# A table load, two chunks on single banks and an order of four products in a two-layer encoder

## The chip, the cores and the metric

The kernel runs on one core of a Trainium2 chip. TensorE (PE in the profile) multiplies, VectorE (DVE) and ScalarE (ACT) prepare operands and take results out of PSUM, GpSimd (POOL) does small things, SyncE (SP) issues nearly all transfers. The metric is device time in microseconds. The kernel before took 2409.35 us, the median of 3 runs (2408.86 to 2410.06).

## The reference

Two layers over 256 tokens of width 2048, in float32. Each layer is a token mixer and a gated MLP, both behind an RMSNorm and added to the residual; a last RMSNorm follows.

```
for layer in range(2):
    hn = rmsnorm(h, norm_mix_g[layer])
    mix = mlstm_mixer(hn, ...) if layer == 0 else hgrn_mixer(hn, ...)
    h = h + mix
    h = h + conv_glu(rmsnorm(h, norm_ffn_g[layer]), ...)
return rmsnorm(h, final_g)
```

The mLSTM mixer projects to q, k, v, an output gate and 32 input and forget gates, runs a matrix memory in both directions for 8 heads, and projects back. The HGRN mixer projects to q, v, an output gate and two forget gates, runs a gated linear recurrence in both directions for 16 heads, and projects back. conv_glu is `(gelu(conv3(u_a)) * u_v) @ w_down` with 5504 inner columns.

## The kernel before

**Products in two parts.** Every big product is made from float32 operands that are split into a rounded high part and the rest: `x = xh + xl`, `w = wh + wl`, and `xh wh + xh wl + xl wh` is accumulated. ACT casts wh from the raw weights (L161, L190 in the first chunk), DVE subtracts to get wl (L162, L191). A piece is 1024 columns of wh and wl; four pieces can be live. SP brings the raw weights, two pieces to a transfer.

**Chunks and pairs.** `stream` walks a list of chunks. A token chunk ("tm", L366 to L368) makes 512 output columns for both halves of the tokens, three products of 512 columns for each half and slice of 128 inputs. A feature chunk ("fm", L382 and L385) makes 256 output features f = 0, 1 for all tokens: for each slice k of 16 and each f a high product (wh against xh and xl side by side, 512 columns) and a low one (wl against xh, 256 columns). These two are called a pair of products below; a slice is two of them. With `turns=1`, which the mLSTM query chunks have, slice 1 is sent high, high, low, low instead (L374, L376): a turn. A `Pair` chunk (`stream_pair`, L253) makes the MLP's projections by Strassen's scheme with the sums c11 to c22 and m1, m6, m7.

**PSUM.** Eight banks: two double banks (`double`, for chunks and the rows of a pair) and four single ones (`aux`, for m1, m6, m7, transposes pz, small sums pr, and the heads' products pa, pd, py). A tile is handed out again when its readers are done. A pair takes both double banks; at its end DVE adds them into hx (L1154), 1024 columns at a time.

**Side work.** `side` holds generators for the heads, the norms and the gates; `tick` lets them issue instructions between products. `tc` then orders each engine's instructions by a simulated timeline, so a changed dependency changes orders, too; instructions on one engine run in that order.

**The start.** ACT issues the transfer of the first slice of x (hx, 128 KB) and the first 16 columns of the small parameters (pp, 8 KB). ACT's first activation needs its function table, whose load stands ahead of it. SP issues the first chunk's weights and the rest of x in groups of 1, 2, 4, 4 and 4 slices (`FIRST`). `prepare(k)` splits slice k of x (L390 on ACT, L391 on DVE) and of the weights. TensorE fills the time with `IDLE` products of ones (L1183), each of which the trace shows as two records.

**HGRN heads.** A head gathers q and k for seven levels (DVE), then sends small products: pa (64 rows) and pd (32 rows, L914), and later py (L962). They stand in TensorE's queue between the projections' products.

**The end.** The down projection of the last 11 slices of the MLP makes output columns 0 to 1023 as a pair, 1024 to 1535 as a token chunk, and 1536 to 2047 as the last chunk. The last chunk does its last seven slices for the first half of the tokens, then for the second, 21 products each (L353 to L355), and `half` (L563 to L576) scales and writes out each half.

Of the kernel before, what the change touches and what calls it, by code (L numbers as in the profile page):

```python
# [15 lines left out]
P = 128  # L16
# [35 lines left out]
AHEAD = 3  # L52
SQUARES = (10, 12, 14, 15)
FIRST = (0, 1, 2, 4, 8, 12, 16)
IDLE = 11

QUAD = 32
LEVELS = (1, 2, 4, 8, 16, 32, 64)
# [5 lines left out]
def trunk_kernel(ctx, tc, xT, x_d, fg_d, pp_d, cst_d, sel_d, w_gate, w_first, w_aq, w_ak, w_av, w_ao, w_aout,  # L64
# [30 lines left out]

    class Side:
        def __init__(self):
            self.now, self.jobs = 0.0, []

        def push(self, gen, stay=False):  # L100
            self.jobs.append([gen, self.now, stay])
# [24 lines left out]

    class Chunk:
        def __init__(self, kind, src, nk, x, done, before=None, last=False, turns=0):
            self.last, self.turns = last, turns
            self.kind, self.src, self.nk, self.x, self.done, self.before = kind, src, nk, x, done, before  # L130
            self.width = {"fm": 256, "tm": 512, "first": 512}[kind]

# [32 lines left out]
    def first_chunk(ch, norm, fetch):  # L165

        raws = [slot(k, "first").bitcast(F32) for k in range(KT)]
        nc.scalar.dma_start(hx[:, 0:1], xT[:, 0:1])
        nc.scalar.dma_start(pp[:, 0:KT], pp_d[:, 0:KT])
        for k0, k1 in zip(FIRST, FIRST[1:]):  # L170
            for k in range(k0, k1):
                nc.sync.dma_start(raws[k], ch.src[:, k * 512:(k + 1) * 512])
            if k0:
                nc.sync.dma_start(hx[:, k0:k1], xT[:, k0:k1])
        rg = wpool.tile([P, 2048], F32, tag="raw", bufs=RAW, name="raw")
        nc.sync.dma_start(rg[:, :512], w_gate)
        late(cst[:, 0:C_LV], cst_d[:, 0:C_LV])
        late(cst[:, C_LV:C_LV + P], sel_d)
        late(pp[:, KT:], pp_d[:, KT:])
        pin = tc.keep_in_program_order  # L180
        d = double("mm")
        ps = [d[:, 0:512], d[:, 512:1024]]
        ws = {}

        def prepare(k):
            norm.take(k, hT[k], pin)
            if k % 2 == 0:
                ws[k] = [wpool.tile([P, 1024], F32R, tag=n, bufs=WB, name=n) for n in ("wh", "wl")]
            wh, wl = [w[:, k % 2 * 512:k % 2 * 512 + 512] for w in ws[k - k % 2]]
            pin(act.copy(wh, raws[k]))  # L190
            pin(dve.tensor_tensor(wl, raws[k], wh.bitcast(F32), ALU.subtract))  # L191
        for k in range(AHEAD):
            prepare(k)
        for k in range(KT):
            if k + AHEAD < KT:
                prepare(k + AHEAD)
            if k in SQUARES:
                for i, q in enumerate(SQUARES):
                    if q == k:
                        ch.squares(i)  # L200
            if k >= KT - LOOK:
                fetch()
            x, (wh, wl) = norm.xs[k], [w[:, k % 2 * 512:k % 2 * 512 + 512] for w in ws[k - k % 2]]
            for t in range(2):
                xh, xl = x[:, t * P:(t + 1) * P], x[:, T + t * P:T + (t + 1) * P]
                pe.matmul(ps[t], xh, wh, start=k == 0, stop=False)
                pe.matmul(ps[t], xh, wl, start=False, stop=False)
# [12 lines left out]
        ch.done(ps + [pg])  # L220
# [98 lines left out]
    def stream(chunks):  # L319
# [10 lines left out]
        for ch in chunks[1:]:  # L330
            if ch.before:
                ch.before()
            if ch.kind == "pair":
# [2 lines left out]
                    return ready.pop(0)  # L336
                stream_pair(ch, take)
                continue
            d = double("mm")
            ps = [d[:, 0:512], d[:, 512:1024]]  # L340
            k = 0
            while k < ch.nk:
                fetch()
# [15 lines left out]
                for kk in range(n):  # L359
                    x = ch.x(k)  # L360
                    st, sp = k == 0, k == ch.nk - 1
                    if ch.kind != "fm":
                        c = slice(kk * 512, (kk + 1) * 512)
                        for t in range(2):
                            xh, xl = x[:, t * P:(t + 1) * P], x[:, T + t * P:T + (t + 1) * P]
                            pe.matmul(ps[t], xh, wh[:, c], start=st, stop=False)  # L366
                            pe.matmul(ps[t], xh, wl[:, c], start=False, stop=False)  # L367
                            pe.matmul(ps[t], xl, wh[:, c], start=False, stop=sp)  # L368
                        side.tick(1.3)
                    else:  # L370
                        if k == 1 and ch.turns:
                            cs = [slice(kk * ch.width + f * P, kk * ch.width + (f + 1) * P) for f in range(2)]
                            for f in range(2):
                                pe.matmul(ps[f], wh[:, cs[f]], x, start=False, stop=False)  # L374
                            for f in range(2):
                                pe.matmul(ps[f][:, 0:T], wl[:, cs[f]], x[:, 0:T], start=False, stop=False)  # L376
                            side.tick(0.65)
                            k += 1
                            continue
                        for f in range(len(ps)):  # L380
                            c = kk * ch.width + f * P
                            pe.matmul(ps[f], wh[:, c:c + P], x, start=st, stop=False)  # L382
                            if f:
                                side.tick(0.325 * len(ps))
                            pe.matmul(ps[f][:, 0:T], wl[:, c:c + P], x[:, 0:T], start=False, stop=sp)  # L385
                    k += 1
# [439 lines left out]
    def hgrn(norm, nxt, after):  # L826
# [60 lines left out]
        def head(hd):  # L887
# [54 lines left out]
            for i in reversed(range(FINE)):  # L942
                product(pd[:, (i + 1) * 64:(i + 2) * 64], *ms[i], QUAD)
            product(pd[:, 0:64], ks, q, QUAD)
            act.copy(AD, both(pd[:, 0:64]))
            for i in range(FINE):
                dve.copy_predicated(AD, mask[i], both(pd[:, (i + 1) * 64:(i + 2) * 64]))
# [41 lines left out]
        for qd in range(BH // 4):  # L989
# [14 lines left out]
            for i in range(6):  # L1004
                if i == 3:
                    chunks.append(Chunk("tm", w_bv[qd], KT, norm.x, done_v))
                def done_i(ps, i=i, qd=qd):
                    for f in range(2):
                        r = 2 * i + f
                        take(4 * qd + r // 3, r % 3, ps[f])  # L1010
                chunks.append(Chunk("fm", w_bq[6 * qd + i], KT, norm.x, done_i, begin if not chunks else None))
            for j in range(4):
                heads[4 * qd + j]["qd"] = four
            chunks.append(Chunk("tm", w_bg[qd], KT, norm.x, done_g))
# [15 lines left out]
    def ffn(layer, norm, nxt):  # L1030
# [78 lines left out]
        for part, (f0, nf) in enumerate(PARTS):  # L1109
# [55 lines left out]
            if final:  # L1165
# [5 lines left out]
                for c in (2, 3):  # L1171
                    chunks.append(Chunk("tm", w_last[c - 2], nf, GT.get, done))
                chunks[-1].last, chunks[-1].half = True, nxt.half
        return chunks, begin, stack.close


# [16 lines left out]
    def swap():  # L1193
        close0()
        b()
    c[0].before = swap
    chunks += c
    chunks += f1
    stream(chunks)
# [97 lines left out]
```

## Time and profile before

| | |
|---|---|
| median of 3 runs | 2409.35 us |
| profiled execution, its own time | 2410.66 us |
| its span | 2408.9 us |
| mean granted TensorE clock | 0.999 |

The span reaches from the first to the last instruction of the profile, the time holds what lies around it as well: 1.76 us here. In the timeline's rows stand the start in us, the duration, the engine, the line of the kernel, the operation and its tiles, and in brackets how long the engine had been idle and what ended that. Matmuls are pipelined: the distance from one start to the next is the pace, and the durations, whose ends are modelled, are longer than it. PEld is TensorE's weight load.

By the timeline the first chunk ends near 34 us, HGRN's projections begin at 1102.53 us, and the last chunk's second half begins at 2395.42 us.

### The profile page before, as it was taken

The numbers are of one execution on the slowest core, as the hardware profiler recorded it, in microseconds if no ns is written. First come the engines' busy times: TensorE is split into PE (matmuls) and PEld (weight loads), VectorE is DVE, ScalarE is ACT, GpSimd is POOL, SyncE is SP. The second block draws the span as 40 slices with busy tenths as digits, with TensorE's granted clock in tenths as the row PEclk, the third lists the DMA queues.
The fourth block names the chain that finished last, engine by engine and source line by source line (L and its number), as shares of the span: only waits on it lengthen the run. The fifth ranks groups of instructions, "written<-read, shape, count | busy, mean of one in ns | idle before, by whom it ended". The sixth has DMA issues, their size and how long they took to land.

```text
span 2408.9 us, 34452 instructions
## 1 busy us (share of the span) xinstructions
PE 2391.3 (99%) x13163; PEld 1998.5 (83%) x13163; DVE 2017.9 (84%) x3009; ACT 1396.1 (58%) x2062; POOL 162.9 (7%) x223
## 2 busy tenths in 40 slices
PE   9999999999999999999999999999999999999998
PEld 7888888788887888888888888888878888888896
DVE  7766667998889887997888888886898889988886
ACT  6655455666456555665555555556566556654664
POOL 0100000000000000001222222220000000000000
PEclk9999999999999999999999999999999999999999
DMA  7655554555555555565555455455555555555564
GB/s 294 200 173 173 190 175 175 194 182 201 192 192 192 192 194 208 165 204 178 173 171 167 171 176 171 162 175 177 190 177 208 181 205 191 193 191 192 192 210 140
DMA packets 67061, 451.01 MB, mean 187 GB/s; under 512 B 7744, under 2 KB 8384, under 8 KB 15440
## 3 DMA queue, kind: packets, MB, share of 16 engines
q1 hardware_dynamic: 64800, 442.32, 52.9%
q0 software_dynamic: 1232, 5.31, 1.0%
q8 instruction: 103, 1.69, 0.3%
q10 hardware_dynamic: 864, 1.19, 0.2%
q14 instruction: 62, 0.51, 0.1%
HBM read 446.62 MB, written 2.16 MB: 186 GB/s over the span
## 4 chain that ended last, share of the span: by engine, by line
PE 92%; DVE 6%; issue 1%; ACT 1%; DMA 0%; POOLq 0%; ACTq 0%; POOL 0%; DVEq 0%
PE c L253 44%; PE mm L382 10%; PE mm L366 7%; PE mm L367 7%; PE mm L368 7%; PE m L253 5%; PE mm L385 5%; DVE wl L162 3%; PE pt L1062 1%; PE pn L731 1%; PE pd L914 1%; PE py L962 1%; DVE T L235 1%; PE pz L476 0%; PE pa L914 0%
## 5 line engine op out<-in xcount | busy, mean ns | idle before, releaser
L162 DVE TENSOR_TENSOR wl<-raw,wh 128x1024 fp32r<-128x1024 f32 (+1 forms) x837 | 967.5, 1167 | 227.5 <-ACT wh L161 226.7
L161 ACT CAST wh<-raw 128x1024 fp32r<-128x1024 f32 (+1 forms) x837 | 829.0, 1001 | 567.7 <-PE c L253 220.1
L253 PE MATMUL c<-wh,xt 128*128 128x512 f32 (+1 forms) x1944 | 620.0, 386 | 0.0
L253 PEld LDWEIGHTS c<-wh,xt 128*128 128x128 f32 x1944 | 363.8, 188 | 71.3 <-ACT wh L161 4.8
L253 PE MATMUL c<-wl,xt 128*128 128x512 f32 (+1 forms) x972 | 374.9, 386 | 0.0
L382 PE MATMUL mm<-xt,wh 128*128 128x512 f32 x1016 | 358.2, 396 | 1.6 <-DVE hx L1154 1.0
L253 PE MATMUL c<-wh,g 128*128 128x512 f32 x1028 | 325.3, 390 | 0.0
L385 PE MATMUL mm<-xt,wl 128*128 128x256 f32 x1016 | 286.6, 282 | 0.0
L161 ACT CAST wh<-T 128x1024 fp32r<-128x1024 f32 (+1 forms) x158 | 161.2, 1039 | 187.2 <-PE c L253 157.9
L382 PEld LDWEIGHTS mm<-xt,wh 128*128 128x128 f32 x1016 | 190.5, 188 | 45.0 <-issue 2.3
L253 PEld LDWEIGHTS c<-wh,g 128*128 128x128 f32 x1028 | 192.8, 188 | 41.2 <-ACT wh L161 1.2
L253 PEld LDWEIGHTS c<-wl,xt 128*128 128x128 f32 x972 | 182.5, 188 | 39.3 <-DVE wl L162 5.1
L162 DVE TENSOR_TENSOR wl<-T,wh 128x1024 fp32r<-128x1024 f32 (+1 forms) x158 | 188.1, 1206 | 31.1 <-ACT wh L161 22.8
L253 PE MATMUL c<-wl,g 128*128 128x512 f32 x514 | 200.9, 391 | 0.0
L253 PE MATMUL c<-wh,F 128*128 128x512 f32 (+1 forms) x500 | 196.0, 395 | 0.8 <-ACT wh L161 0.8
L385 PEld LDWEIGHTS mm<-xt,wl 128*128 128x128 f32 x1016 | 191.6, 189 | 1.3
L366 PE MATMUL mm<-wh,xt 128*128 128x512 f32 x480 | 188.0, 392 | 0.0
L367 PE MATMUL mm<-wl,xt 128*128 128x512 f32 x480 | 187.8, 391 | 0.0
L368 PE MATMUL mm<-wh,xt 128*128 128x512 f32 x480 | 187.3, 390 | 0.0
L253 PE MATMUL m<-wh,F 128*128 128x512 f32 (+1 forms) x316 | 116.9, 395 | 0.0
L253 PEld LDWEIGHTS c<-wl,g 128*128 128x128 f32 x514 | 96.5, 188 | 21.3 <-DVE wl L162 1.4
L253 PEld LDWEIGHTS c<-wh,F 128*128 128x128 f32 x500 | 94.0, 188 | 20.3 <-ACT wh L161 1.6
(271 smaller groups left out, 3332.9 us busy)
## 6 DMA issues: line engine op xcount, KB each, us to landing
raw<-in_w_up SPq DMA_DIRECT2D x160, 1024.0 KB, 4.7
raw<-in_w_down SPq DMA_DIRECT2D x79, 1024.0 KB, 4.8
raw<-in_w_bq SPq DMA_DIRECT2D x48, 1024.0 KB, 5.2
raw<-in_w_ao SPq DMA_DIRECT2D x16, 1024.0 KB, 4.8
raw<-in_w_aout SPq DMA_DIRECT2D x16, 1024.0 KB, 4.8
raw<-in_w_bv SPq DMA_DIRECT2D x16, 1024.0 KB, 4.8
raw<-in_w_bg SPq DMA_DIRECT2D x16, 1024.0 KB, 4.7
raw<-in_w_bout SPq DMA_DIRECT2D x16, 1024.0 KB, 4.8
```

The source lines that it names most:

```text
L161: act.copy(wh[:, :m], r)
L162: dve.tensor_tensor(wl[:, :m], r, wh[:, :m].bitcast(F32), ALU.subtract)
L235: dve.tensor_tensor(T4[:, 0:2 * w].rearrange("p (a b) -> p a b", a=2), b12, raw[:, w:3 * w].rearrange("p (a b) -> p a b", a=2), ALU.subtract)
L253: pe.matmul(acc[name][:, 0:w], a, b, start=name not in begun, stop=sp and i == 2)
L366: pe.matmul(ps[t], xh, wh[:, c], start=st, stop=False)
L367: pe.matmul(ps[t], xh, wl[:, c], start=False, stop=False)
L368: pe.matmul(ps[t], xl, wh[:, c], start=False, stop=sp)
L382: pe.matmul(ps[f], wh[:, c:c + P], x, start=st, stop=False)
L385: pe.matmul(ps[f][:, 0:T], wl[:, c:c + P], x[:, 0:T], start=False, stop=sp)
L731: pe.matmul(pn[:, 0:258], w, v, start=(i == 0), stop=(i == len(parts) - 1))
L914: pe.matmul(pd[o:o + w, c:c + w], k[:, b * w:(b + 1) * w], q[:, e * w:(e + 1) * w], start=True, stop=True)
L962: pe.matmul(py[:, c], AT[:, s if s == t else 2 + s], V[:, s, j * P:(j + 1) * P], start=(s == 0), stop=(s == 1))
```

## The change

Five edits:

1. The transfer of pp is issued ahead of that of hx, and ACT copies two columns of a constant into a scratch tile (`warm`) behind these issues, so the table is loaded there. There are 12 idle products instead of 11.
2. The first HGRN chunk, behind the last pair of the first MLP, takes two single banks (`apart`) in place of a double bank.
3. So do the two last chunks of the kernel, of which the first stands behind a pair.
4. All HGRN feature chunks get `turns=1`.
5. Behind a head's small products the next slice of a feature chunk is sent as a turn, too (`side.turned`).

```diff
-IDLE = 11
+IDLE = 12
...
+        nc.scalar.dma_start(pp[:, 0:KT], pp_d[:, 0:KT])
         nc.scalar.dma_start(hx[:, 0:1], xT[:, 0:1])
-        nc.scalar.dma_start(pp[:, 0:KT], pp_d[:, 0:KT])
+        warm = ev.tile([P, 2], F32, tag="rs", bufs=6, name="warm")
+        tc.keep_in_program_order(act.copy(warm, hmx))
...
-            d = double("mm")
-            ps = [d[:, 0:512], d[:, 512:1024]]
+            if ch.apart:
+                ps = [aux("mm") for _ in range(2)]
+            else:
+                d = double("mm")
+                ps = [d[:, 0:512], d[:, 512:1024]]
...
-                        if k == 1 and ch.turns:
+                        if k == 1 and ch.turns or side.turned:
+                            side.turned = False
                             cs = [slice(kk * ch.width + f * P, kk * ch.width + (f + 1) * P) for f in range(2)]
                             for f in range(2):
-                                pe.matmul(ps[f], wh[:, cs[f]], x, start=False, stop=False)
+                                pe.matmul(ps[f], wh[:, cs[f]], x, start=st, stop=False)
                             for f in range(2):
-                                pe.matmul(ps[f][:, 0:T], wl[:, cs[f]], x[:, 0:T], start=False, stop=False)
+                                pe.matmul(ps[f][:, 0:T], wl[:, cs[f]], x[:, 0:T], start=False, stop=sp)
...
             product(pd[:, 0:64], ks, q, QUAD)
+            side.turned = True
...
-                chunks.append(Chunk("fm", w_bq[6 * qd + i], KT, norm.x, done_i, begin if not chunks else None))
+                chunks.append(Chunk("fm", w_bq[6 * qd + i], KT, norm.x, done_i, begin if not chunks else None, turns=1))
...
                 chunks[-1].last, chunks[-1].half = True, nxt.half
+                chunks[-1].apart = chunks[-2].apart = True
...
     c[0].before = swap
+    c[0].apart = True
```

ACT's first instructions, before:

```order
L168 DMA hx<-in_xT 128x256
L169 DMA pp<-in_pp 128x16
L390 ACT_TABLE_LOAD
L390 ACTIVATE xt_151<-hx,pp 128x256
L190 CAST wh<-first_106 128x512
```

and now:

```order
L168 DMA pp<-in_pp 128x16
L169 DMA hx<-in_xT 128x256
L171 ACT_TABLE_LOAD
L171 COPY warm<-mhalf 128x2
L396 ACTIVATE xt_154<-hx,pp 128x256
L192 CAST wh<-first_107 128x512
```

The two issues have changed places, and the table load belongs to the copy, which reads a constant, where it belonged to the first activation, which reads hx and pp.

TensorE in the first HGRN chunk, before (mm_9494 is this chunk's double bank, xt6 and xt7 are slices of x, pz are transposes that make slices 8 to 15):

```order
L382 MATMUL mm_9494<-xt6_9304,wh_9430 128x512
L476 MATMUL pz_9554<-cst_71,hx_75 128x128 x4
L476 MATMUL pz_9565<-cst_71,hx_75 128x128 x4
L385 MATMUL mm_9494<-xt6_9304,wl_9431 128x256
L382 MATMUL mm_9494<-xt7_9307,wh_9430 128x512
```

and now (mm_9497 and mm_9498 are this chunk's single banks, mm_9658 is the next chunk's double bank):

```order
L388 MATMUL mm_9658<-xt7_9310,wh_9585 128x512
L391 MATMUL mm_9658<-xt7_9310,wl_9586 128x256
L482 MATMUL pz_9558<-cst_71,hx_75 128x128 x4
L482 MATMUL pz_9569<-cst_71,hx_75 128x128 x4
L388 MATMUL mm_9497<-xt9_9536,wh_9451 128x512
L391 MATMUL mm_9497<-xt9_9536,wl_9452 128x256
```

The last eight transposes stood behind slice 6 of the first chunk and stand behind slice 7 of the next chunk now, since two of the four single banks are taken; the two chunks' slices 8 to 11 are mixed behind them.

TensorE in the last chunk as changed (mm_21821 is the first half of the tokens, mm_21822 the second, g6 to g8 are slices of the gated values):

```order
L360 MATMUL mm_21821<-wh_21823,g7_21213 128x512
L358 MATMUL mm_21821<-wh_21841,g8_21476 128x512
L360 MATMUL mm_21822<-wh_21805,g4_21109 128x512
L358 MATMUL mm_21822<-wh_21805,g5_21144 128x512
L359 MATMUL mm_21822<-wl_21806,g5_21144 128x512
L360 MATMUL mm_21822<-wh_21805,g5_21144 128x512
L358 MATMUL mm_21822<-wh_21823,g6_21184 128x512
L359 MATMUL mm_21821<-wl_21842,g8_21476 128x512
```

Before, all products of the first half stood ahead of all of the second. Now seven of the second half's stand among the first half's, and 14 behind them.

More of the change, by code (lines that the diff above doesn't have):

```diff
@@ L97, in __init__ @@
         def __init__(self):
-            self.now, self.jobs = 0.0, []
+            self.now, self.jobs, self.turned = 0.0, [], False
         def push(self, gen, stay=False):
@@ L128, in __init__ @@
         def __init__(self, kind, src, nk, x, done, before=None, last=False, turns=0):
-            self.last, self.turns = last, turns
+            self.last, self.turns, self.apart = last, turns, False
             self.kind, self.src, self.nk, self.x, self.done, self.before = kind, src, nk, x, done, before
```

## The prediction

> **What bounds the kernel now.** I read the first part of the page and the chain of waits first, then the waits of TensorE alone (PE: engine, line, what it waited for, us in total, times, longest).
>
> ```profile
> span 2408.9 us, 34452 instructions
> PE 2391.3 (99%) x13163; PEld 1998.5 (83%) x13163; DVE 2017.9 (84%) x3009; ACT 1396.1 (58%) x2062; POOL 162.9 (7%) x223
> PE 92%; DVE 6%; issue 1%; ACT 1%; DMA 0%; POOLq 0%; ACTq 0%; POOL 0%; DVEq 0%
> ...
> PE mm L206 <- ACT wh L190: 1.7, 1, 1.7
> PE mm L382 <- DVE hx L1154: 1.0, 1, 1.0
> PE mm L366 <- DVE hx L1154: 0.9, 1, 0.9
> PE mm L353 <- DVE hx L563: 0.8, 1, 0.8
> PE mm L382 <- issue: 0.7, 1, 0.7
> ```
>
> TensorE is busy 99% of the span, so only its own gaps and a slower pace of its own instructions can be won. The listed gaps come to 5.1 us, and four of the five belong to places that the change touches. 0.2% of the time, about the least that a measurement of this kernel tells from no change, is 4.8 us: the change has to take nearly everything to reach it.
>
> **The start.** The timeline (start, duration, engine, line, operation, idle before it):
>
> ```profile
> 0.73 0.41 ACTq L168 DMA_DIRECT2D hx<-in_xT  x1
> 1.09 4.83 PE L1183 MATMUL idle<-ones 128*128 128x128 f32 x22 [1.09 <-POOL ones L1177]
> 1.17 0.46 ACTq L169 DMA_DIRECT2D pp<-in_pp  x1
> 5.25 1.28 ACT L390 ACT_TABLE_LOAD   x1 [5.25 <-DMA pp<-in_pp]
> 6.42 0.68 SPq L174 DMA_DIRECT2D hx<-in_xT  x1
> 7.62 0.50 PE L206 MATMUL mm<-wh,xt 128*128 128x512 f32 x1 [1.69 <-ACT wh L190]
> 8.75 0.51 ACT L390 ACTIVATE xt<-hx,pp 128x256 fp32r<-128x256 f32 x1 [0.27 <-DMA hx<-in_xT]
> 13.72 0.51 ACT L390 ACTIVATE xt<-hx,pp 128x256 fp32r<-128x256 f32 x1 [2.08 <-DMA hx<-in_xT]
> 14.77 0.69 DVE L191 TENSOR_TENSOR wl<-first,wh 128x512 fp32r<-128x512 f32 x1
> 15.29 0.39 PE L206 MATMUL mm<-wh,xt 128*128 128x512 f32 x1
> 15.52 0.19 PEld L207 LDWEIGHTS mm<-wl,xt 128*128 128x128 f32 x1 [0.27 <-DVE wl L191]
> ```
>
> The table load of 1.28 us starts only when pp has landed. With the small copy ahead it runs under the transfers. hx is now issued second: 0.73 to 1.17 is 0.44 later, so the first operand is ready about 1.28 - 0.44 = 0.8 us earlier, and the twelfth idle product (two of 24 records, 4.83 / 22 x 2 = 0.44 us) ends near 6.4, just before the first real product.
>
> I still cost this at **nothing**, because another wait comes after it. Slice k = 4 of x comes with a transfer issued at 6.42 and is there at 13.72; ACT has stood idle 2.08 us by then. DVE's low half of that slice's weights ends at 14.77 + 0.69 = 15.46, and TensorE takes it at 15.52. TensorE came to slice 4 at 15.29 and waited 0.27 for it. A TensorE that starts earlier waits longer at the same spot, since SP's queue, which issues that transfer, is not moved. Bounds: 1.28 gained, if the whole start slides, and 1.7 lost, if the clock falls back (a rival below). I take 0, the value of the wait that ends last.
>
> **Single banks behind the pair, twice, and in the last chunk.** The timeline at the first HGRN chunk, at the second last chunk, and between the halves of the last:
>
> ```profile
> 1100.97 0.39 PE L253 MATMUL c<-wl,g 128*128 128x512 f32 x1
> 1101.17 2.34 DVE L1154 TENSOR_TENSOR hx<-hx,c 128x1024 f32<-128x1024 f32 x2
> 1101.19 0.39 PE L253 MATMUL c<-wh,g 128*128 128x512 f32 x1
> 1102.53 0.47 PE L382 MATMUL mm<-xt,wh 128*128 128x512 f32 x1 [0.95 <-DVE hx L1154]
> ...
> 2367.88 0.39 PE L253 MATMUL c<-wh,g 128*128 128x512 f32 x1
> 2369.22 0.47 PE L366 MATMUL mm<-wh,g 128*128 128x512 f32 x1 [0.95 <-DVE hx L1154]
> ...
> 2394.25 0.39 PE L355 MATMUL mm<-wh,g 128*128 128x512 f32 x1
> 2395.42 0.50 PE L353 MATMUL mm<-wh,g 128*128 128x512 f32 x1 [0.78 <-DVE hx L563]
> 2397.12 0.88 DVE L575 TENSOR_SCALAR hx<-hx,fss 128x512 f32<-128x512 f32 x2 [0.69 <-POOL fss L569]
> 2398.49 0.35 ACTq L576 DMA_DIRECT2D out<-fl  x1
> ```
>
> Products follow each other by 0.22 to 0.23 us (1100.97 to 1101.19). From start to start the three gaps lose 1102.53 - 1101.19 - 0.23 = 1.11, 2369.22 - 2367.88 - 0.23 = 1.11 and 2395.42 - 2394.25 - 0.23 = 0.94 us. In the first two the new chunk wants the double bank that DVE is still adding into hx; with two single banks nothing holds it.
>
> At HGRN what could come in its place is the transposes: two single banks are lent out, so two of the four pz tiles are sent only behind slices 4 to 7 of the next chunk. I followed the new orders from 1101.42 on with durations of rows. TensorE takes 0.69 us for a slice of four products and 0.9 us for eight transposes: the first eight slices and eight transposes end at 1107.9, the next chunk's first four and slice 8 at 1111.4, its slices 4 to 7 at 1114.2, the last eight transposes at 1115.1, three more slices at 1117.2, and then it asks for the first of the four late xt. On ACT two weight casts (1.05 us each) stand ahead of these four, the second of which needs the buffer that slices 4 to 7 leave at 1114.2; it ends at 1115.3, DVE's low half of it (1.22) at 1116.6, and the first late xt (0.48) at 1117.1. It just fits: I take 1.05 of 1.11, bounds 0 and 1.2 (the product behind the gap also takes 0.47 where others take 0.39). At the tail no transposes are left and three weight pieces are ready when the pair ends: 1.1, bounds 0.8 and 1.2.
>
> In the last chunk 7 of the 21 products of the second half are now mixed into the end of the first half, and 14 stand behind it: 14 x 0.227 = 3.2 us. Before, the first half's outputs kept ACT until 2398.49 + 0.35 = 2398.84, that is 4.36 us behind its last product (2394.48); the second half's square, which starts about 1.0 us behind the last product of its half, needs ACT 3.2 + 1.0 = 4.2 us behind it. That costs 0.15 of the 0.94: **0.8**, bounds 0.4 and 0.94.
>
> **High, high, low, low.** Groups of L382 (count, busy, mean ns) in all HGRN projections, in the stretch at 1163 and in the one at 1183; then a turned pair that the kernel has already:
>
> ```profile
> L382 PE MATMUL mm<-xt,wh 128*128 128x512 f32 x768 | 271.7, 396 | 1.6 <-DVE hx L1154 1.0 <-issue 0.7
> ...
> L382 PE MATMUL mm<-xt,wh 128*128 128x512 f32 x19 | 6.7, 398 | 0.0
> ...
> L382 PE MATMUL mm<-xt,wh 128*128 128x512 f32 x45 | 15.6, 391 | 0.0
> ...
> 109.32 0.28 PE L385 MATMUL mm<-xt,wl 128*128 128x256 f32 x1
> 109.44 0.64 PE L374 MATMUL mm<-xt,wh 128*128 128x512 f32 x2
> 109.92 0.40 PE L376 MATMUL mm<-xt,wl 128*128 128x256 f32 x2
> 110.15 0.40 PE L382 MATMUL mm<-xt,wh 128*128 128x512 f32 x1
> ```
>
> There are two paces: a pair takes 7 ns (398 - 391) longer in some stretches. Going through the stretches from break to break, the slow ones begin behind a token chunk (each of five), behind the norm's pr, and behind some transposes and small products; all behind py are fast. About 300 of the 768 pairs are slow: 300 x 7 ns = 2.1 us (upper bound from the first row: 5 ns x 768 = 3.8, but that also counts products that open a run). The mLSTM chunks, which have a turn in slice 1, stay fast behind it. The change sends 38 turned groups in HGRN. By their places about 85 slow pairs stay (between a transpose and the next turn), so 1.5 us is won. A turn costs 110.15 - 109.44 = 0.71 against 2 x 0.347 = 0.69: 38 x 0.016 = 0.6 lost. Net **0.9**, bounds 0.6 lost (no stretch changes) and 1.5 won.
>
> A rule of the Trainium skill speaks against this term ("TensorE: Matmul & The Clock Gate", LDWEIGHTS): a weight load takes its columns over 1.2, 107 ns for 128. By it the load fits under the shorter product (109.32 to 109.44, 120 ns), order could not matter, and the sum would be 3.0 less the turns' cost, 2.4 us. The 398 against 391 says that it does matter; I keep the row.
>
> **The sum.** 0 + 1.05 + 0.9 + 1.1 + 0.8 = 3.85 us. Against the profiled execution's span that is 2408.9 - 3.85 = 2405.05, against its own time 2410.66 - 3.85 = 2406.8. That execution was 1.31 above the median, and holds one gap of its own:
>
> ```profile
> 1536.23 0.50 PE L382 MATMUL mm<-xt,wh 128*128 128x512 f32 x1 [0.69 <-issue]
> ```
>
> The same place in the three other groups of heads has no such gap, and nothing in the change is about it. From the median: 2409.35 - 3.85 = **2405.5 us**.
>
> **Rivals.** The clock rows (window, length, PE busy, ..., granted clock, DMA share, GB/s):
>
> ```profile
> 5.48:8.89 3.41, 1.49 (x7) 0.92 (x6) 1.78 (x4) 3.13 (x6) 0.00 (x0) 1.00 1.01 333
> 8.89:12.30 3.41, 3.41 (x10) 2.60 (x9) 2.57 (x5) 2.75 (x5) 0.00 (x0) 0.51 1.03 360
> ```
>
> 1. The clock falls back behind the wait for slice 4. A stretch with 1.49 of 3.41 us busy was followed by 3.4 us at 0.51. Now TensorE, warm, would do slices 0 to 3 by about 13.1 (slice 2 is held by its transfer until 8.75, the xt row, and six products of 0.227 follow each low half) and stand until 14.8, and again until 15.5: the stretch 12.3 to 15.7 would be about as empty. Half speed for 3.4 us from 15.7 costs 3.4 / 2 = 1.7, with no slack left there: 2407.2. The start rows speak for it, the unknown phase against. The Trainium skill, on the same page ("What's actually happening"), has a free-running window of 3.4 us at whose end the clock is set by how busy it was; the 0.51 row agrees. Chance 0.2.
>
> 2. The start pays after all: the eight transfers under way come in a new order, the slice-4 transfer lands earlier, and up to the 1.28 of the table load is won: 2404.2. For it: SP's queue waits on landings. Against it: the DMA share is 1.01 to 1.03 there, so the bytes, not the issues, set the landing. 0.17.
>
> 3. The transposes become the wait at HGRN: the last four xt come late and give back the 1.05: 2406.5. 0.08.
>
> 4. Slower: turns shift a fast stretch to the slow pace and it keeps that. If all 768 pairs ran slow, 768 x 7 ns = 5.4, less 2.1 paid now, plus 0.6 for turns, is 3.9 lost instead of 0.9 won: 2410.3. It decides once more than some 680 pairs are slow. Against it: the mLSTM turns leave fast stretches. 0.05.
>
> My forecast keeps 0.5. The range 2403.5 to 2408.0 takes in rivals 1 to 3 and the terms' bounds. Faster by over 0.2% (below 2404.5) needs rival 2 or every term at its best: 0.22; slower by over 0.2%: 0.02; between them 0.76.
>
> **What would show it.** The three DVE waits of the first rows must be gone from TensorE's list, with slice 4 of the first chunk still entering at about 15.5. L382's old stretches (now L388) should show 391, except between a transpose and a turn. A granted clock near 0.5 between 15 and 20 us is rival 1; a wait of TensorE for xt around 1115 is rival 3. I am wrong if the first chunk ends over 0.5 us earlier, or if slow stretches follow turns.

## The result, and the profile after

| | before | changed |
|---|---|---|
| median | 2409.8 us (22 runs, 2408.5 to 2411.8) | 2405.96 us (22 runs, 2404.6 to 2409.8) |
| ratio to before | | 0.9985, 95% interval 0.9978 to 0.9992 |
| profiled execution, its own time | 2410.66 us | 2404.82 us |
| its span | 2408.9 us | 2403.0 us |

3.84 us less, 0.16%; by the interval 1.9 to 5.3 us less. The two profiled executions are further apart, 5.8 us: that of before holds a gap that is not its rule (0.69 us at 1536.23), and that of the changed kernel is near the fast end of its runs.

The first part of the page, and the waits of TensorE, of the changed kernel (engine, line, what it waited for, us in total, times, longest):

```profile
span 2403.0 us, 34456 instructions
PE 2389.1 (99%) x13165; PEld 1997.6 (83%) x13165; DVE 2017.9 (84%) x3009; ACT 1396.5 (58%) x2063; POOL 163.6 (7%) x223
...
PE pt L1069 <- DVE c L1075: 1.8, 6, 0.4
...
PE c L255 <- ACT wh L161: 0.8, 2, 0.4
PE mm L208 <- ACT wh L192: 0.5, 1, 0.5
PE pa L944 <- DVE QK L933: 0.3, 1, 0.3
PE mm L209 <- DVE wl L193: 0.2, 1, 0.2
```

The three waits for hx (1.0, 0.9 and 0.8 us) are gone. One wait is new: pa for QK. The start, HGRN's first chunk and the tail in the timeline:

```profile
1.65 1.28 ACT L171 ACT_TABLE_LOAD   x1 [1.65 <-PEq L1301]
3.67 1.87 SPq L174 DMA_DIRECT2D first<-in_w_first  x4
5.59 0.43 SPq L176 DMA_DIRECT2D hx<-in_xT  x1
11.81 0.51 ACT L396 ACTIVATE xt<-hx,pp 128x256 fp32r<-128x256 f32 x1 [1.18 <-DMA hx<-in_xT]
12.88 0.50 PE L208 MATMUL mm<-wh,xt 128*128 128x512 f32 x1 [0.54 <-ACT wh L192]
24.71 1.93 PE L217 MATMUL gates<-hx,raw 128*32 128x256 f32 x32
...
1099.55 0.39 PE L255 MATMUL c<-wh,g 128*128 128x512 f32 x1
1099.78 0.39 PE L388 MATMUL mm<-xt,wh 128*128 128x512 f32 x1
1155.10 0.46 PE L944 MATMUL pa<-QK 128*128 128x128 f32 x2 [0.27 <-DVE QK L933]
...
2393.95 0.39 PE L360 MATMUL mm<-wh,g 128*128 128x512 f32 x1
2394.44 0.68 DVE L569 TENSOR_TENSOR hx<-hx,mm 128x512 f32<-128x512 f32 x1
2395.01 0.35 ACTq L582 DMA_DIRECT2D out<-fl  x1
2395.41 0.63 ACT L586 ACTIVATE jk<-hx 128x512 f32<-128x512 f32 x1 [0.43 <-DVE hx L569]
2398.41 0.34 ACTq L582 DMA_DIRECT2D out<-fl  x1
```

The whole kernel can be cut at four marks that all the traces have: the start of the gate products behind the first chunk (26.64 us before, 24.71 now), the first product behind the token chunk that ends HGRN's first group (1162.69, 1160.13), the same mark three groups of heads later (1535.04, 1531.99), and the last product (2400.09, 2393.95). From there to the last issue it is 4.15 us before (2404.24 - 2400.09) and 4.46 now. The lengths between these marks, in all the traces of this study:

| kernel | gates at | to HGRN's mark | three groups | to the last product |
|---|---|---|---|---|
| before | 26.64 | 1136.05 | 372.35 | 865.05 |
| pp issued first alone | 27.24 | 1136.17 | 372.35 | 864.22 |
| table load early alone | 25.65 | 1135.98 | 372.36 | 864.17 |
| whole new start alone | 25.07 | 1135.97 | 372.35 | 865.56 |
| turns alone | 26.36 | 1135.98 | 371.85 | 865.44 |
| single banks alone | 26.39 | 1135.32 | 372.35 | 861.92 |
| changed kernel | 24.71 | 1135.42 | 371.86 | 861.96 |
| changed kernel, again | 26.04 | 1135.50 | 372.04 | 862.11 |
| fewer turns | 25.93 | 1135.41 | 371.79 | 861.71 |
| cut start, all turns | 23.75 | 1135.57 | 372.69 | 862.50 |
| cut start, all turns, again | 23.99 | 1135.52 | 371.85 | 861.90 |
| cut start, fewer turns | 23.88 | 1135.42 | 371.80 | 861.77 |
| cut start, no turn in each third chunk | 24.23 | 1135.50 | 372.14 | 862.58 |
| cut start, no new turns | 24.18 | 1135.57 | 372.35 | 861.79 |

The last column of before holds its gap of 0.69 us, and the 372.69 a gap of 0.48; the rest of the last column's scatter, 0.6 to 1.4 us, is one late transfer (below). Otherwise a column moves by tenths, mostly with the edit that belongs to it, where the scatter of whole runs is a whole microsecond. The same kernel can differ by 0.2, though (371.86 and 372.04 for the changed kernel), so smaller steps are not told apart. That table is what the experiments are read by. The whole times alone can't do it: most intervals of a ratio below are 0.0009 to either side, which is 2.2 us.

### The profile page after: what moved, and what is told of

Same layout as the page of the kernel before. It is cut to its first block, busy times and chain, and to the rows that moved or that the text cites. A ratio compares the mean times of both kernels' runs of the same rounds, so it can differ in the third digit from the quotient of the medians.

```text
span 2403.0 us, 34456 instructions
## 1 busy us (share of the span) xinstructions
PE 2389.1 (99%) x13165; PEld 1997.6 (83%) x13165; DVE 2017.9 (84%) x3009; ACT 1396.5 (58%) x2063; POOL 163.6 (7%) x223
## 4 chain that ended last, share of the span: by engine, by line
PE 91%; DVE 7%; issue 1%; ACT 1%; DMA 0%; SPq 0%; POOLq 0%; POOL 0%; ACTq 0%; DVEq 0%
PE c L255 44%; PE mm L388 9%; PE mm L371 7%; PE mm L372 7%; PE mm L373 7%; PE m L255 5%; PE mm L391 4%; DVE wl L162 3%; PE pt L1069 1%; PE mm L380 1%; PE pn L737 1%; PE pd L920 1%; PE py L969 1%; DVE T L237 1%; PE pz L482 0%
## 5 line engine op out<-in xcount | busy, mean ns | idle before, releaser
L388 PE MATMUL mm<-xt,wh 128*128 128x512 f32 x940 | 331.9, 396 | 0.0
L391 PE MATMUL mm<-xt,wl 128*128 128x256 f32 x940 | 264.3, 281 | 0.0
L388 PEld LDWEIGHTS mm<-xt,wh 128*128 128x128 f32 x940 | 176.4, 188 | 38.7
L391 PEld LDWEIGHTS mm<-xt,wl 128*128 128x128 f32 x940 | 177.0, 188 | 0.8
```

## The experiments

Theory A: the start is set by SP's queue, whose ninth transfer waits for the first one that was issued. Theory B: it is set by the table load. My prediction said that neither edit moves it.

**pp issued first, alone.**

```diff
-        nc.scalar.dma_start(hx[:, 0:1], xT[:, 0:1])
         nc.scalar.dma_start(pp[:, 0:KT], pp_d[:, 0:KT])
+        nc.scalar.dma_start(hx[:, 0:1], xT[:, 0:1])
```

> The kernel before with pp issued ahead of hx, and nothing else (no copy that loads the table early, 11 idle products). Theory A (the issue queue): SP's ninth transfer waits for the landing of the first one that was issued, and pp lands sooner than hx, so SP goes on at about 3.7 instead of 4.45 us, slice 4 of x is split at about 11.8 to 12.3 instead of 13.72, and the gate products of the first chunk, at 26.71 before, start 1.2 to 1.7 us earlier although the table load is still in the way; the time is 1.2 to 1.7 us less. Theory B (the table load sets the start): slice 4 stays near 13.7, the gate products within 0.3 us of 26.7, the time the same. My prediction (the transfer of slice 4 is not moved by anything here): as theory B.

Measured: 2409.37 us against 2410.02 of the kernel before beside it, ratio 0.9997 (0.9988 to 1.0006). Of its trace, the timeline and the clock row (the last three numbers are the granted clock, the DMA share and GB/s):

```profile
7.29 0.79 PE L206 MATMUL mm<-wh,xt 128*128 128x512 f32 x1 [1.14 <-ACT wh L190]
10.32 0.63 PE L206 MATMUL mm<-wh,xt 128*128 128x512 f32 x1
10.74 0.63 PE L207 MATMUL mm<-wl,xt 128*128 128x512 f32 x1
12.04 0.51 ACT L390 ACTIVATE xt<-hx,pp 128x256 fp32r<-128x256 f32 x1 [1.08 <-DMA hx<-in_xT]
```

```profile
8.89:12.30 3.41, 3.41 (x9) 2.64 (x9) 2.07 (x5) 2.33 (x5) 0.00 (x0) 1.00 1.01 351
```

The first half of A holds. SP's queue went on at 3.83 where it had waited to 4.45, and slice 4 was there at 12.04 instead of 13.72. But nothing came of it, since TensorE then did nearly all of its products 0.42 us apart (10.32 to 10.74) from 7.29 to 13.7, nearly twice the usual 0.227. So the gate products came at 27.24, later than before. The pace is that of half the clock, though the clock column reads 1.00 all the while. The column is no evidence here: this trace holds no clock record ahead of 13.78 us, where the clock is recorded as full. In every trace the column reads 1.00 up to the first record (4.2 to 6.9 us in the others), and up to there the idle products run 0.213 us apart; those behind it, where there are any, run 0.11 to 0.13 apart. The Trainium skill ("TensorE: Matmul & The Clock Gate", Wait — 56ns, not 53.3ns?) gives 426.7 ns from start to start for 512 columns on a cold array; the 0.42 here agrees with it.

**The early table load and the twelfth idle product, alone.**

```diff
-IDLE = 11
+IDLE = 12
...
+        warm = ev.tile([P, 2], F32, tag="rs", bufs=6, name="warm")
+        tc.keep_in_program_order(act.copy(warm, hmx))
```

> The kernel before with the copy that loads the table early and 12 idle products, but hx still issued ahead of pp. Theory A: SP's ninth transfer still goes at 4.4 us, slice 4 at 13.5 to 13.9, gate products within 0.3 us of 26.7, time the same within 0.5 us; TensorE starts near 6.3 and waits over 1 us for slice 4. Theory B: gate products and time 1.2 to 1.7 us earlier. My rival 1 (clock): a granted clock near 0.5 between 15.7 and 19.1 us, and the gate products up to 1.7 us later.

Measured: 2409.48 us, ratio 0.9998 (0.9989 to 1.0007). Slice 4 at 12.77, full pace from the first product on, gate products at 25.65. SP's queue went on at 4.23, as theory A said, but the gate products came 0.7 to 1.0 us earlier than in the three traces with the old start (26.36 to 26.64), which A had not expected; B had expected 1.2 to 1.7. Neither theory fits both runs.

**The whole new start, alone:** both of these edits together.

> All edits of the start alone: pp first, the early table load, 12 idle products. Both theories: gate products about 1.6 us earlier than 26.71, as in the profile of the change, the time 1.3 to 1.8 us less than before. My prediction: nothing.

Measured: 2409.03 us, ratio 0.9996 (0.9987 to 1.0005). Slice 4 at 12.17, full pace, gate products at 25.07, 1.57 us earlier than before. And yet its span is only 1.2 us shorter. Its last column in the table tells where the rest went; its VectorE and TensorE in the second MLP's down projection:

```profile
2159.57 1.23 DVE L237 TENSOR_TENSOR T<-raw 128x1024 f32<-128x1024 f32 x1 [2.87 <-DMA raw<-in_w_down]
2167.47 0.50 PE L255 MATMUL c<-wl,g 128*128 128x512 f32 x1 [0.37 <-DVE wl L162]
2169.54 0.50 PE L255 MATMUL c<-wl,g 128*128 128x512 f32 x1 [0.40 <-DVE wl L162]
```

One transfer of 1 MB took 7.5 us here from issue to landing; the median of those at this place in the trace before is 4.9. VectorE waits for this one in every trace, from 0.3 to 2.9 us. Up to 1.6 us the last column shows nothing of it; with 1.8, 2.1, 2.6 and 2.9 us of waiting it is 0.6 to 1.4 us longer. The long wait occurred with the old start, too (2.6 us, turns alone), and in the changed kernel, with the new start, it was 0.3 once and 1.6 once, so it is chance and no effect of the start.

**The turns alone**, edits 4 and 5 of the change on the kernel before:

```diff
+                        if k == 1 and ch.turns or side.turned:
...
+            side.turned = True
...
+                chunks.append(Chunk("fm", w_bq[6 * qd + i], KT, norm.x, done_i, begin if not chunks else None, turns=1))
```

> The turns alone. By my prediction's term: 0.9 us less time in HGRN, and between the first HGRN product and the last one before the output projection 0.85 to 0.9 us less in the profile. By the profile of the change (three of four last feature chunks of a group of heads run at the slow pace behind their turn, 0.3 us each): 0.3 to 0.6 us less. By my rival 4: up to 3.9 us more.

Measured: 2409.53 us, ratio 0.9998 (0.9989 to 1.0007). The three groups took 371.85 instead of 372.35: 0.50 won, where the prediction's term was 0.9 for all of HGRN.

**The single banks alone**, edits 2 and 3 (three chunks: one in HGRN, two at the end):

```diff
+            if ch.apart:
+                ps = [aux("mm") for _ in range(2)]
...
+                chunks[-1].apart = chunks[-2].apart = True
...
+    c[0].apart = True
```

> The kernel before with single banks alone: the chunk behind the pair of HGRN and the two last chunks of the MLP; start and turns as before. My theory (each side waits for its own bank only): the wait of TensorE for hx at the first chunk of HGRN (0.9 to 1.0 us) goes, the two waits of 0.8 and 0.3 to 0.4 us at the end go, and the last addition starts 0.4 us behind the last product where it started 0.4 us behind it already, so the gain at the end comes from the first half of the work on hx that no longer waits for the second side. Together 2.9 us less (0.95 + 1.9): 2407.1 us where the kernel before takes 2410.0. Rival (the late transposes are uncovered in place of the wait): 0.9 us at HGRN is not won, 2408.0. In the trace the HGRN chunk arrives at the same time as before (1102.4 to 1102.6), and the turn rows do not change: slow excess of the feature pairs 2.0 to 2.4 us.

Measured: 2407.14 us against 2410.25, ratio 0.9989 (0.9980 to 0.9997): 3.1 us less, where 2.9 was expected. By the marks it is 2.7: HGRN's stretch is 0.7 shorter than before, the last one 2.3 shorter than the two undisturbed ones with a double bank (864.2), and behind the last product 0.3 is given back. At HGRN the wait for hx went, and this came:

```profile
1156.66 0.46 PE L941 MATMUL pa<-QK 128*128 128x128 f32 x2 [0.53 <-DVE QK L930]
```

All nine traces with single banks wait here, for 0.27 to 0.55 us; none of the five with a double bank does. VectorE is busy without a pause from 1140 to 1157 in both kinds. TensorE gained 1.1 us on it and gives a quarter to a half of that back at the first place where it needs VectorE's newest result.

**The changed kernel again, with fewer turns, and with the start's fourth set of transfers cut in two.** The second leaves out the turns in four of the six feature chunks of a group:

```diff
-                chunks.append(Chunk("fm", w_bq[6 * qd + i], KT, norm.x, done_i, begin if not chunks else None, turns=1))
+                chunks.append(Chunk("fm", w_bq[6 * qd + i], KT, norm.x, done_i, begin if not chunks else None, turns=int(i in (0, 3))))
```

and the third changes the transfers:

```diff
-FIRST = (0, 1, 2, 4, 8, 12, 16)
+FIRST = (0, 1, 2, 4, 6, 8, 12, 16)
```

> The changed kernel once more, unaltered, beside the two above on the same chip: 2406.0 us (2405.2 to 2406.5 as a median). In its trace the first set of x lands as before, gate products 24.5 to 25.1; three stretches of 95 feature products behind py at the slow pace (0.30 us each) if theory P holds, at other places if R does. For the weight transfer of the down projection near 2155 us, which took 4.9 to 5.1 us in two traces and 7.3 to 7.5 in two others: if it is chance, VectorE waits 0.3 to 2.9 us for it here as well; if the new start sets it, the wait is that of the first trace of this kernel, 0.3.

Measured: 2406.37 us, ratio 0.9984 (0.9975 to 0.9993). Its trace has the gate products at 26.04, not at 24.71:

```profile
13.14 0.51 ACT L396 ACTIVATE xt<-hx,pp 128x256 fp32r<-128x256 f32 x1 [2.39 <-DMA hx<-in_xT]
```

Slice 4 is there 1.3 us later than in the first trace of the same kernel. So the start's gain has a chance in it. With the old start the gate products came at 26.36, 26.39 and 26.64 (mean 26.46), with the new one at 24.71, 25.07, 25.93 and 26.04 (mean 25.44): 1.0 us earlier, between 0.3 and 1.9.

The nine traces whose fourth set is whole, side by side. SP's time is that of its issue behind the first eight transfers, and half pace means products 0.42 to 0.43 us apart in the first chunk:

| kernel | pp first | table early | SP goes on | slice 4 split | products at half pace | gates at |
|---|---|---|---|---|---|---|
| before | no | no | 4.45 | 13.72 | 7 | 26.64 |
| turns alone | no | no | 4.32 | 13.20 | 6 | 26.36 |
| single banks alone | no | no | 4.26 | 13.43 | 8 | 26.39 |
| pp issued first alone | yes | no | 3.83 | 12.04 | 12 | 27.24 |
| table load early alone | no | yes | 4.23 | 12.77 | 0 | 25.65 |
| whole new start alone | yes | yes | 3.85 | 12.17 | 0 | 25.07 |
| changed kernel | yes | yes | 3.67 | 11.81 | 0 | 24.71 |
| changed kernel, again | yes | yes | 4.29 | 13.14 | 0 | 26.04 |
| fewer turns | yes | yes | 3.91 | 12.98 | 0 | 25.93 |

There are two limits. In eight of the nine the gate products come 12.9 to 13.2 us behind the split of slice 4, so its landing sets the start, and it is earlier with pp first: 12.4 in the mean against 13.3, though the two ranges overlap. In the ninth, pp issued first alone, TensorE itself is late: with the late table load it waits 1.1 to 2.1 us for its first product and then runs at half pace. So in these traces the new order pays only with the early table load. How the 1.0 us divides between the two, they can't tell, nor whether it is the early load or the twelfth idle product, which always come together, that keeps the half pace away.

> The changed kernel with the first chunk's fourth set of transfers cut in two: raw slices 4 and 5 and their x of 256 KB, then 6 and 7 and theirs, one transfer more on SP's queue. Theory A (the start is set by when x of slice 4 lands, and that by the bytes and the issue ahead of it): xt of slice 4 at 9.9 to 10.9 us where the changed kernel has 11.81, TensorE does not wait there (0.54 + 0.22 + 0.2), the gate products start 0.9 to 1.0 us earlier (23.7 to 23.8 where it has 24.7). Theory B (it is the count of transfers in flight: one more issue waits for one more landing): xt of slice 4 within 0.4 us of 11.81, or x of slice 6 becomes late in its place, and the gate products start at 24.5 to 25.2.

Measured: 2405.63 us, ratio 0.9981 (0.9973 to 0.9990). Slice 4 at 10.66 without any wait of ACT, gate products at 23.75: theory A's numbers. (Here A and B are those of this expectation.) In four more traces with this cut they came at 23.88 to 24.23. A transfer that brings only what is needed next took the wait and most of the chance out of the start.

> The changed kernel with turns only in feature chunks that stand directly behind a chunk of tokens (two of six in each group of heads) and behind the small products pd; 20 turns fewer or so. Theory P (the turn in the last feature chunk of a group flips three stretches of 95 products from 391 to 398 ns a pair): the stretches behind py are fast again, 3 x 0.27 = 0.8 us less, and the stretches behind chunks of tokens stay fast; slow excess of the feature pairs 0.8 to 1.0 us where the changed kernel has 1.7. 2405.2 us where the changed kernel takes 2406.0. Theory R (the pace of a stretch is set by where the instructions happen to fall, and not by the turn): other stretches become slow, excess 1.5 to 2.3, and the time stays within 0.3 us.

Measured: 2405.50 us, ratio 0.9980 (0.9971 to 0.9989), 0.9 under the changed kernel beside it. The three stretches of 95 products are fast again, as P expected, but a fourth one, at 1182 us, became slow, and by the table the three groups are only 0.07 to 0.25 us shorter than with all turns, where P had 0.8.

**The turns once more, all on the cut start.** With all of them:

> The changed kernel with the fourth set cut in two, as run before (turns in all six feature chunks of a group): the comparison for the three below, which have the same start and the same single banks. 2405.6 us. Gate products at 23.6 to 24.4 us if cutting the set takes the chance out of the start (it gave 23.8 once), or 24.5 to 26 if that single trace was luck, as the uncut start gave 24.7 to 26.0. Three stretches of 95 products behind py slow by 0.30 us each.

2405.65 us, ratio 0.9983 (0.9974 to 0.9992), with the three stretches slow again. In the first and fourth feature chunk only:

> The same with turns only in the first and fourth feature chunk of each group (directly behind a chunk of tokens). Theory P (each stretch's pace is a fixed result of the order in it): the same stretches as in the trace with the uncut start and these turns, one behind py slow in the first group of heads (0.31) and the pd and pz ones by 0.05 to 0.13, slow excess 0.9 to 1.05, and 0.7 us less than with all turns: 2404.9 us. Theory R (chance): the slow stretches lie elsewhere, time within 0.3 us of that with all turns.

2404.33 us, ratio 0.9979 (0.9970 to 0.9988): the best of the study, 5.5 us under the kernel before and 1.3 under the same start with all turns. The runs of the two overlap (up to 2405.8 here, from 2404.4 there). The same seven stretches are slow as with these turns on the uncut start, as this form of P said. Without the one in the third chunk:

```diff
-                chunks.append(Chunk("fm", w_bq[6 * qd + i], KT, norm.x, done_i, begin if not chunks else None, turns=1))
+                chunks.append(Chunk("fm", w_bq[6 * qd + i], KT, norm.x, done_i, begin if not chunks else None, turns=int(i != 2)))
```

> The same with turns in all feature chunks but the third of each group, which is the one that theory P blames: four turns fewer than with all of them. P: the three slow stretches of 95 products lose their 0.3 us, everything else keeps its pace, slow excess 1.7 - 0.8 = 0.8 to 0.9, time 0.8 us less than with all turns: 2404.8 us. If the pace of the stretch is already decided at its start, behind py, and not at the turn: the excess stays at 1.6 to 1.8 and so does the time.

2405.01 us, ratio 0.9981 (0.9972 to 0.9990). The three stretches stayed slow. This run does not test P as I meant it to: by the places of the turns in the trace, the stretches of 95 products belong to the fifth and sixth chunks of a group, and the third chunk's turn stands elsewhere (at 1249.2 us in the changed kernel). What it did show is that without that turn the stretch at 1253 is slow (0.12 us in 36 products) where it was fast with it. Without new turns:

```diff
-            side.turned = True
...
-                chunks.append(Chunk("fm", w_bq[6 * qd + i], KT, norm.x, done_i, begin if not chunks else None, turns=1))
+                chunks.append(Chunk("fm", w_bq[6 * qd + i], KT, norm.x, done_i, begin if not chunks else None))
```

> The same without turns but those that the kernel before has: start (cut) and single banks alone. Slow excess as in the kernel before, 1.95 to 2.3 us, in rows of 0.10 to 0.13 behind chunks of tokens, pd and pz. My prediction gave the turns 0.9 us net; the traces read so far give 0.4 to 0.5: so 0.4 to 0.5 us more than with all turns, 2406.1 us (2406.5 by the prediction's figure). If the turns give nothing on balance, the same time as with all of them.

2405.67 us, ratio 0.9984 (0.9975 to 0.9992): as much as with all turns, though the three groups take 372.35 against 371.85.

P's first form, that the turn in the last chunk flips the 95 products, falls by the traces themselves. Groups of L388 in the changed kernel (count, busy, mean ns), the 95 products behind py at 1181, and those at 1305:

```profile
L388 PE MATMUL mm<-xt,wh 128*128 128x512 f32 x46 | 16.0, 393 | 0.0
...
L388 PE MATMUL mm<-xt,wh 128*128 128x512 f32 x45 | 16.0, 399 | 0.0
```

Each holds one turn, some 35 products in. The first is fast on both sides of it, the second slow from its first product on. So the turn there flips nothing; the pace was settled at the break, behind py. With turns in two chunks it is the other way round, the stretch at 1180 slow and that at 1303 fast, and neither holds a turn:

```profile
L388 PE MATMUL mm<-xt,wh 128*128 128x512 f32 x47 | 16.6, 399 | 0.0
...
L388 PE MATMUL mm<-xt,wh 128*128 128x512 f32 x46 | 16.0, 392 | 0.0
```

In shorter stretches a turn does change the pace. In the changed kernel, ahead of the turn at 1249.2 and behind it:

```profile
L388 PE MATMUL mm<-xt,wh 128*128 128x512 f32 x10 | 3.5, 394 | 0.0
...
L388 PE MATMUL mm<-xt,wh 128*128 128x512 f32 x9 | 3.2, 398 | 0.0
```

At 1175.1 it likewise goes from fast to slow. At 1298.8 it ends fast, where the same stretch without that turn (fewer turns) is slow to its end.

Nor is the pace fixed by the order alone. The two executions of the changed kernel, which send the same instructions, behind pd at 1238 in the first and at 1239.5 in the second:

```profile
L388 PE MATMUL mm<-xt,wh 128*128 128x512 f32 x17 | 6.0, 392 | 0.0
...
L388 PE MATMUL mm<-xt,wh 128*128 128x512 f32 x17 | 6.0, 398 | 0.0
```

This stretch and one at 1229 are the only ones in the four groups that differ between the two, and they make most of the 0.18 us between 371.86 and 372.04. The two executions with the cut start and all turns differ at the same two places. In the first group, the 140 products behind the norm's pr (at 1113 us) take 353 ns a pair in the traces of before and of pp issued first alone, and 347 in those of the table load early alone and of the whole new start alone; TensorE's order there is the same in all four. So P's second form (the order fixes each pace) and R (chance) both hold in part: most stretches keep their pace from execution to execution, some do not.

What is common to the places was not found. One pattern has no exception: where turns are sent behind pd, the 95 products behind the next py run at the other pace than the products ahead of that py (32 places in eight traces). Two things are the same in every trace that has them: behind a token chunk the stretch is fast where it begins with turns and slow where it does not, and all six kernels without new turns take 372.35 or 372.36 us for the three groups.

## Why the prediction was right, and where it was not

The time was 2405.96, forecast 2405.5, and 3.84 us were won, forecast 3.85. That agreement is luck: one term was too small by 1.0 us and two too large by 0.45 and 0.5, and they cancelled. Both signs that the prediction gave for being wrong came: the first chunk ended over 0.5 us earlier, and slow stretches follow turns.

| term | predicted | by the marks |
|---|---|---|
| start | 0 | 1.0 (0.3 to 1.9) |
| HGRN's first chunk | 1.05 | 0.6 |
| turns | 0.9 | 0.4 |
| tail, both parts | 1.1 + 0.8 | 2.3 - 0.3 = 2.0 |
| sum | 3.85 | 4.0 |

**The start failed**, at the step "since SP's queue, which issues that transfer, is not moved". That the wait for slice 4 sets the start held in eight of nine traces; that it stays where it was did not, since the queue is moved. The wait of SP's queue at the issue behind the first eight transfers, in the trace of before and in that of the changed kernel (its releaser, us, times, longest):

```profile
SPq L172 <- DMA hx<-in_xT: 0.9, 1, 0.9
```

```profile
SPq L174 <- DMA pp<-in_pp: 0.2, 1, 0.2
```

SP waits for the landing of the transfer that was issued first of all, and in all 14 traces goes on 0.01 to 0.02 us behind it; whether the program or the chip sets that limit is not shown. That transfer was hx, 128 KB, and is now pp, 8 KB. So the four weights ahead of slice 4's x went out at 3.67 instead of 4.45, and that x at 5.59 instead of 6.42. The order of two issues on ACT set the time of the queue on SP. My argument against it, that a DMA share of 1.01 to 1.03 lets only the bytes count, does not hold: with the same bytes slice 4 came 0.9 us earlier in the mean. It isn't sure in a single execution: in the changed kernel's second trace pp itself landed late, SP went on at 4.29, and slice 4 came at 13.14. This was rival 2, to which I gave 0.17. It left out the other half, what the early table load (with its twelfth idle product) does for TensorE: all four traces with the late load have half pace in the first chunk, with the first product 1.1 to 2.1 us behind the idle ones, and none of ten with the early load has it, with at most 0.8 us there. A size was off, too: the first operand came 1.5 us earlier (its split at 5.03 instead of 6.55), not 0.8. I had taken off 0.44 for the later issue of hx, but the old table load waited for pp.

**HGRN was over-sized.** The wait of 1.11 us went whole, and the late transposes fitted, as the step said: between 1115 and 1117 TensorE waits for no xt. But I followed the order only to 1117.1. VectorE's chain for the first pa, 40 us further on, was not in the working, and that is where 0.3 to 0.55 us went. It is rival 3's kind, at another place and half the price.

**The turns were over-sized.** That order has a hand in the pace stands: 398 against 391 ns, and stretches behind token chunks went fast in all seven places, worth some 0.7 us. The step that failed is "about 85 slow pairs stay": by the distances of the products some 230 were slow in the changed kernel. I had no term for stretches that turn slow: three of 95 products (0.3 us each), and shorter ones. The price of the turns was too high in return: one took some 4 ns more than the pairs in its place, not 16, which is 0.15 us for all and not 0.6. Rival 4 had the effect, at 0.05 and as all or nothing; it occurs in part, and takes half of the term. (Its 680 pairs come from no sum: the other terms' 2.95 us would be gone at 636, where 636 x 7 ns is 2.95 + 1.5.) By the marks 0.50 is won in the three groups and about 0.1 lost in the last; the whole times (-0.5 us for turns alone, none on the cut start) can't tell 0.4 from nothing. The weight-load rule of the Trainium skill ("TensorE: Matmul & The Clock Gate", LDWEIGHTS) gives 107 ns for a load of 128 columns. What the prediction drew from it, that order could cost nothing, does not agree with these traces; nor does the rule tell why the same loads in the same order show 399 and 392 ns.

**The tail was right** to 0.1 us, with the cost that was named: ACT's square of the second half now starts behind the first half's last issue (2395.01 + 0.35, then 2395.41), so the last issue follows the last product by 4.46 us instead of 4.15, 0.31 more, where I had written 0.15. The row's bracket names VectorE's sum, but that ended at 2394.44 + 0.68 = 2395.12; of the 0.31, 0.07 is the sum's later start and 0.24 ACT's wait for its own issue. **Rival 1** did not come: the clock rows of the changed kernel, from the wait on,

```profile
12.30:15.71 3.41, 2.65 (x11) 1.95 (x11) 3.34 (x7) 3.41 (x9) 0.00 (x0) 1.00 1.04 404
15.71:19.12 3.41, 3.41 (x17) 2.83 (x16) 3.37 (x7) 3.41 (x7) 0.00 (x0) 1.00 1.05 397
```

show 2.65 of 3.41 us busy and full clock behind it; slice 4 had landed earlier than I had assumed. That alone is not the reason: with slice 4 at 13.14 (the second trace) the stretch was 1.57 us busy, and the next was at full pace all the same.

What stays open: why a stretch takes one pace or the other, and the 1.3 us between all turns and two per group on the cut start, of which the marks show some 0.4 (0.1 at the start, 0.1 up to HGRN's mark, 0.05 in three groups, 0.13 behind them).

## What to carry to other kernels

Follow each transfer back to the issue that its queue waits for: with eight under way, the order of the first two, on another engine's queue, decided when the ninth could go, and cutting one set so that its first slices come alone was worth 1.4 us in the mean (five traces against four), more than either edit to the start alone. Then ask whether the engine is ready by then: here it ran at half pace in every trace without the early table load and its twelfth idle product. When a wait of the bounding engine is removed, look for the next place where it needs the engine that it has just overtaken, even 50 us on; a quarter to a half of the gain went there. And compare edits of a few tenths between marks in the trace, not by whole times: here one late transfer in the down projection moved a run by up to 1.4 us.

## What was not expected of the hardware

- The same kernel has its start 1.3 us apart in two executions (gate products at 24.71 and 26.04) through the landing of one 512 KB transfer; two transfers of 256 KB in its place gave 23.75 to 24.23 in five executions.
- Products ran at half pace (0.42 us for 512 columns, from 7.29 to 13.7 us) while the clock column showed 1.00; that trace has no clock record ahead of 13.78 us.
- A pair of products has two paces, 7 ns apart, that mostly last from one break to the next. A turn can change it both ways or not at all, the 95 products without any turn ran at either, and two executions of the same kernel have two of their stretches at different paces.
